# Two-layer retention and block-attention trunk: the weights' columns interleaved in memory by 16-byte lines, and read by TensorE in four strided passes

## The chip, the cores and the metric

The kernel runs as one program on one core of a Trainium2 chip. The metric is the device time of one execution in microseconds (us), and lower is better.

## What is computed

The reference is a decoder trunk of two layers over 256 tokens of width 1024, in float32. Cut to what matters here, it reads:

```python
for i in range(DEPTH):                                   # 2 layers
    h = rms_norm(x, norm_g[i])
    proj = h @ w_in[i]                                   # (256,1024) @ (1024,4096)
    rq, rk, rv, rz, mq, mk, mv, mz = jnp.split(proj, cuts, axis=-1)
    r_out = silu(rz) * retention(rotary(rq), rotary(rk), rv, ret_norm_g[i])
    m_out = silu(mz) * moba(rms_norm(mq, q_norm_g[i]), rms_norm(mk, k_norm_g[i]), mv, rel_bias)
    x = x + jnp.concatenate([r_out, m_out], -1) @ w_out[i]          # (1024,1024)
    gate = sigmoid(rms_norm(x) @ w_ple_gate[i])                     # (1024,1024)
    x = x + gate * rms_norm(p[i] @ w_ple[i], ple_norm_g[i])         # (256,1024)
```

With 256 tokens the block attention is plain causal attention inside one block, with a bias that depends on the distance of the two tokens. Nearly all arithmetic lies in the four weight products: `w_in`, `w_out`, `w_ple` and `w_ple_gate`.

## The kernel before

Tokens are handled in two row blocks of 128 (`m`), the width of 1024 in eight blocks of 128 (`k`), and output columns in groups of 512. To keep the precision of float32, each operand of a weight product is split into a high part (rounded to `fp32r`) and a low part (what is left), and three matmuls are added in PSUM: high by high, high by low, low by high. The function `mm3` (lines 364 to 372) issues these three. In each, the stationary operand is a 128x128 block of the activations (`a`), loaded into TensorE by an LDWEIGHTS that goes with each matmul, and the moving operand is 128 rows by 512 columns of the split weights (`wh` or `wl`), read in the order of its columns.

A weight travels in pieces of 512 KB (two `k` blocks of 512 columns). SyncE issues its load into one of eight staging buffers `wst` (line 320), ScalarE copies it to `wh` with rounding (line 330), VectorE subtracts to get `wl` (line 333), and TensorE then uses it for twelve matmuls. There are five `wh`/`wl` pairs; in some stretches buffers of the attention part (`T`, `V`, `G`, `PS`, `K2`) are lent to the weights as well, which is why the profile shows matmuls that read `T`, `G` or `K`. A last piece of the second layer is done with 256 columns at a time. The input projection of the first layer's first group starts from smaller loads (`in_early`), which `first_block`, `late_columns`, `key_block` and `first_rows` handle (lines 409 to 518): the first 128x512 block comes as two halves of 256 columns, its copy to `wh` is done in two casts (lines 427 and 444), and the first four real matmuls are 256 columns wide.

Between the weight products lie the attention and retention parts: small matmuls of 128 and 256 columns into `mix` (lines 894, 912, 922, 972), which read no weights. Activations are transposed by DMA on SyncE's queue (line 595).

The order of all instructions is set by a planner in the kernel itself, the class `Flow`, which keeps a clock for each engine. Each step of a chain says on which engine it runs, what it is assumed to cost, and what buffers it takes; the planner issues the steps in the order in which they would come ready. TensorE's clock moves by `ROW` for each matmul of 512 columns (`ROW = 0.227`, in us), by 0.53 of it at 256 columns in `mm3`, and by `TILE`, twelve rows, for the due time of a weight piece. The attention parts are put between the weight products by `tick()`, once their inputs have been ready, by the planner's clocks, for a margin. These costs decide the order of the instructions alone; on the chip semaphores hold each instruction until its inputs are there.

Of the kernel before, what the change touches and what calls it, by code (L numbers as in the profile page):

```python
# [52 lines left out]
PE, ACT, DVE, POOL, SP = range(5)  # L53
ROW = 0.227
TILE = 12 * ROW
# [182 lines left out]
def ask(eng, cost, take=(), after=(), mb=None):  # L238
    return eng, cost, take, after, mb
# [3 lines left out]
def tile_hybrid_trunk(ctx: ExitStack, tc: tile.TileContext, early, x, pT, ple_g, rel_bias,  # L243
# [106 lines left out]
    class Parts:  # L350
# [10 lines left out]
        def need(self, m, k):  # L361
            if (m, k) in self.made:
                flow.need(self.made.pop((m, k)))

    def mm3(ps, a, m, k, stage, kk, start, stop, cols=slice(0, GW)):
        a.need(m, k)
        wh, wl = stage.part(kk // 2)[kk % 2]
        ah, al = a.of(m, k)
        flow.row(3 * ROW * (1.0 if cols.stop - cols.start == GW else 0.53))
        nc.tensor.matmul(ps, ah, wh[:, cols], start=start, stop=False)  # L370
        nc.tensor.matmul(ps, ah, wl[:, cols], start=False, stop=False)  # L371
        nc.tensor.matmul(ps, al, wh[:, cols], start=False, stop=stop)  # L372

# [35 lines left out]
    def first_block(k, home, at):  # L409
        b = home[:, at:at + BLOCK]  # L410
        w = b[:, :GW] if k else home[:, at:at + 2 * FIRST].rearrange("p (t n) -> p t n", t=2)[:, :, :S]
        src = b[:, GW:] if k else home[:, at + S:at + 2 * S]
# [10 lines left out]
        if k:  # L423
            nc.scalar.copy(hi, w)
            firsts[k, "lo"] = flow.begin(first_low(k, w, hi, lo), k - 19.7, flow.end + HOP)
        else:
            nc.scalar.copy(hi[:, :S], w[:, 0])
            firsts["split"] = [v.rearrange("p (t n) -> p t n", t=2) for v in (hi, lo)]
        g = gains["g"][:, Q_NG + k:Q_NG + k + 1]
# [8 lines left out]
    def late_columns(home):  # L438
        w = home[:, :2 * FIRST].rearrange("p (t n) -> p t n", t=2)[:, :, :S]
        yield ask(SP, 0.43, mb=S / 2048)  # L440
        nc.sync.dma_start(w[:, 1], early_block("late"))
        yield ask(ACT, 0.36)
        hi, lo = firsts["split"]
        nc.scalar.copy(hi[:, 1], w[:, 1])
        firsts[0, "lo"] = flow.begin(first_low(0, w, hi, lo), -19.7, flow.end + HOP)
# [52 lines left out]
    def first_rows(k, ps, start, stop, key=()):  # L498
# [9 lines left out]
        for i, (which, w, c) in enumerate(order):  # L508
# [3 lines left out]
            for j, sl in enumerate([slice(0, S), slice(S, GW)] if halves else [slice(0, GW)]):  # L512
                if j:
                    flow.need(firsts["late"])
                for m in range(MT):
                    flow.row(0.12 if halves else ROW)
                    nc.tensor.matmul(ps[m][:, sl], (a0.lo if which[0] == "lo" else a0.hi)[:, k, m * P:(m + 1) * P],  # L517
                                     w[:, sl], start=start and i + j == 0, stop=stop and i == 2)

# [157 lines left out]
    def embed(l):  # L677
# [22 lines left out]
        for m in range(MT):  # L700
            ps = [bank(mix_p, "mix") for _ in range(2)]
            for n in range(2):
                for k, (wh, wl) in enumerate(w.part(n)):
                    ah, al = (v[:, k, m * P:(m + 1) * P] for v in (ph, pl))
                    flow.row(3 * ROW)
                    nc.tensor.matmul(ps[n], ah, wh, start=k == 0, stop=False)  # L706
                    nc.tensor.matmul(ps[n], ah, wl, start=False, stop=False)  # L707
                    nc.tensor.matmul(ps[n], al, wh, start=False, stop=k == 1)  # L708
                if m:
# [24 lines left out]
    def layer(l, aT):  # L734
        last = l == DEPTH - 1
        T, TC, V, G, VC, GC = {}, {}, {}, {}, {}, {}
        K2, Q2 = {}, {}

        def stats(m):
            return ST_X[l, m, "v"]  # L740
# [85 lines left out]
        def value(g, m, ps):  # L826
            yield ask(ACT, 0.585, take=() if m else ("V",), after=need_stats(m))
            if not m:
                V[g] = big.tile([P, MT, GW], F32, name="V", bufs=1)
            nc.scalar.activation(V[g][:, m], ps, AF.Copy, scale=stats(m)[0 if g == MV else 2])  # L830
            flow.free("acc")
# [432 lines left out]
```

## Time and profile before

| | |
|---|---|
| device time, median of 3 runs | 303.85 us (303.44 to 304.65) |
| the profiled execution: span from first to last instruction | 301.7 us |
| what lies around the span, against the median | 2.1 us (303.85 - 301.7) |
| granted TensorE clock over the span | 1.000 of full speed |
| TensorE matmuls, share of the span busy | 98% (1411 instructions) |
| VectorE, ScalarE, GpSimd busy | 84%, 72%, 11% |
| DMA, mean rate | 231 GB/s, 69.77 MB |

The profiled execution's own device time is not listed apart from the three runs, so its span is set beside their median, and the 2.1 us around it are taken as constant. In the rows of the profile, PE is TensorE's matmul, PEld its weight load (the stationary operand), DVE is VectorE, ACT ScalarE, POOL GpSimd, SP SyncE, and SPq the DMA issues on SyncE's queue. A matmul's time in a row runs from its start until its result is through; matmuls overlap, so what one costs in a row of them is the distance from one start to the next. A row such as `ACT wh L330 <- PE acc L372: 11.6, 13, 1.7` says that line 330 on ScalarE waited 11.6 us in all for line 372 on TensorE, 13 times, 1.7 us the longest.

### The profile page before, as it was taken

To read this page: it belongs to the slowest core of one execution; us is meant where nothing else is said; L and a number is where in the kernel's file an instruction comes from. 1 tells how busy PE (TensorE), PEld (TensorE's weight loads), DVE (VectorE), ACT (ScalarE), POOL (GpSimd) and SP (SyncE) were. 2 spreads that over 40 slices of the span, in tenths; PEclk is the share of its full clock that TensorE was granted. 3 is DMA by queue.
4 is the path that set the end of the run, shared out by engine and by line. 5 is a ranking of instruction groups with operands and counts; after the bars stand their busy time and mean duration, and the time that the engine had idled before them with its cause. 6 is when DMAs were issued, how large, how long until landed. Compare 5 with 4: busy or idle time off the path is not lost.

```text
span 301.7 us, 4301 instructions
## 1 busy us (share of the span) xinstructions
PE 296.9 (98%) x1411; PEld 248.5 (82%) x1411; DVE 253.6 (84%) x461; ACT 215.9 (72%) x376; POOL 32.5 (11%) x44
## 2 busy tenths in 40 slices
PE   8999999999999999999999999999999999999994
PEld 5888888888888888888888888888898888888884
DVE  4959799899899997899997489999978797969832
ACT  4789963889656985997793796699646869389211
POOL 6005200000001200031012220000000030002200
PEclk9999999999999999999999999999999999999999
DMA  7999989978769676896779769798997777833011
GB/s 236 366 405 411 276 241 379 303 243 184 237 205 297 266 194 228 179 295 245 250 198 293 243 187 227 258 218 175 281 323 184 252 223 185 276 73 70 1 72 70
DMA packets 61774, 69.77 MB, mean 231 GB/s; under 512 B 46260, under 2 KB 47160, under 8 KB 61624
## 3 DMA queue, kind: packets, MB, share of 16 engines
q1 hardware_dynamic: 61712, 69.50, 77.3%
q8 instruction: 11, 0.18, 0.2%
q14 instruction: 11, 0.09, 0.1%
q0 software_dynamic: 32, 0.01, 0.0%
q10 hardware_dynamic: 8, 0.00, 0.0%
HBM read 57.42 MB, written 1.05 MB: 194 GB/s over the span
## 4 chain that ended last, share of the span: by engine, by line
PE 98%; DVE 0%; ACT 0%; issue 0%
PE acc L371 26%; PE acc L372 26%; PE acc L370 26%; PE acc L517 5%; PE mix L922 4%; PE mix L894 2%; PE mix L278 1%; PE mix L708 1%; PE mix L707 1%; PE mix L371 1%; PE mix L370 1%; PE mix L372 1%; PE mix L706 1%; PE mix L972 1%; PE mix L912 1%; ACT tmp L1144 0%
## 5 line engine op out<-in xcount | busy, mean ns | idle before, releaser
L370 PE MATMUL acc<-wh,a 128*128 128x512 f32 (+1 forms) x286 | 110.4, 386 | 0.0
L371 PE MATMUL acc<-wl,a 128*128 128x512 f32 (+1 forms) x286 | 110.1, 385 | 0.0
L372 PE MATMUL acc<-wh,a 128*128 128x512 f32 (+1 forms) x286 | 110.0, 385 | 0.0
L333 DVE TENSOR_TENSOR wl<-wst,wh 128x1024 fp32r<-128x1024 f32 x76 | 91.8, 1217 | 10.4 <-ACT wh L330 10.3
L330 ACT CAST wh<-wst 128x1024 fp32r<-128x1024 f32 x76 | 79.5, 1057 | 21.3 <-PE acc L372 11.6
L372 PEld LDWEIGHTS acc<-wh,a 128*128 128x128 f32 x286 | 53.7, 188 | 10.6
L370 PEld LDWEIGHTS acc<-wh,a 128*128 128x128 f32 x286 | 53.8, 188 | 10.6
L371 PEld LDWEIGHTS acc<-wl,a 128*128 128x128 f32 x286 | 53.8, 188 | 10.5
L585 ACT COPY u<-tok 128x1024 uint16<-128x1024 uint16 x30 | 31.0, 1050 | 11.6 <-DVE tok L940 7.5
L637 POOL TENSOR_TENSOR ro<-rs_t,neghalf 128x4 f32<-128x4 f32 x4 | 5.8, 1459 | 132.2 <-DVE rs_t L635 132.2
L585 ACT COPY u<-x_t 128x1024 uint16<-128x1024 uint16 x12 | 12.5, 1041 | 8.2 <-DVE x_t L1100 6.3
L621 ACT CAST a<-tmp 128x512 fp32r<-128x512 f32 x20 | 12.4, 619 | 7.8 <-DVE tmp L618 5.8
L1144 ACT ACTIVATE tmp<-acc,hr 128x512 f32<-128x512 f32 (+1 forms) x9 | 5.8, 639 | 15.6 <-PE acc L372 15.6
L604 DVE COPY tmp<-w 128x512 uint16<-128x512 uint16 x40 | 16.1, 454 | 0.0
L604 DVE COPY T<-w 128x512 uint16<-128x512 uint16 x32 | 12.6, 455 | 2.2 <-DMA w<-u 2.2
L623 DVE TENSOR_TENSOR a<-tmp,a 128x512 fp32r<-128x512 f32 x20 | 13.7, 683 | 0.0
L1147 DVE SCALAR_TENSOR_TENSOR tmp<-tmp,E 128x512 f32<-128x512 f32 (+1 forms) x9 | 5.7, 629 | 8.5 <-ACT tmp L1144 8.5
L517 PE MATMUL acc<-wh,a 128*128 128x512 f32 (+1 forms) x42 | 11.7, 401 | 0.0
L922 PEld LDWEIGHTS mix<-V,PS 128*128 128x128 f32 x96 | 11.3, 192 | 0.3
L922 PE MATMUL mix<-V,PS 128*128 128x128 f32 x96 | 11.4, 275 | 0.0
L370 PE MATMUL acc<-T,a 128*128 128x512 f32 (+1 forms) x30 | 11.2, 375 | 0.0
L372 PE MATMUL acc<-T,a 128*128 128x512 f32 (+1 forms) x30 | 11.2, 375 | 0.0
(143 smaller groups left out, 462.3 us busy)
## 6 DMA issues: line engine op xcount, KB each, us to landing
wst<-in_w_in SPq DMA_DIRECT2D x59, 512.0 KB, 6.6
wst<-in_w_out SPq DMA_DIRECT2D x16, 512.0 KB, 7.4
wst<-in_w_gate SPq DMA_DIRECT2D x16, 512.0 KB, 4.3
wst<-in_w_ple SPq DMA_DIRECT2D x4, 512.0 KB, 7.6
wst<-in_early SPq DMA_DIRECT2D x4, 384.0 KB, 6.8
a<-in_early SPq DMA_DIRECT2D x3, 384.0 KB, 5.1
x_t<-in_x SPq DMA_DIRECT2D x1, 1024.0 KB, 11.7
gb<-in_ple_g SPq DMA_DIRECT2D x2, 512.0 KB, 7.2
```

The costliest lines, as they stand in the source:

```text
L330: nc.scalar.copy(hi, s)
L333: nc.vector.tensor_tensor(lo, s, hi.bitcast(F32), op=ALU.subtract)
L370: nc.tensor.matmul(ps, ah, wh[:, cols], start=start, stop=False)
L371: nc.tensor.matmul(ps, ah, wl[:, cols], start=False, stop=False)
L372: nc.tensor.matmul(ps, al, wh[:, cols], start=False, stop=stop)
L517: nc.tensor.matmul(ps[m][:, sl], (a0.lo if which[0] == "lo" else a0.hi)[:, k, m * P:(m + 1) * P], w[:, sl], start=start and i + j == 0, st ...
L585: nc.scalar.copy(u, src.bitcast(U16).rearrange("p (n t) -> p t n", t=2))
L604: nc.vector.tensor_copy(v, w[:, t].rearrange("p (h b) k -> p h (b k)", h=v.shape[1]))
L621: nc.scalar.copy(h, src)
L623: nc.vector.tensor_tensor(a.lo[:, k0:k0 + 4, m * P:(m + 1) * P], src, h.bitcast(F32), op=ALU.subtract)
L894: nc.tensor.matmul(ps, w[a], x[b], start=i == 0, stop=i == 2)
L922: nc.tensor.matmul(ps[:, h * DH:(h + 1) * DH], lhs(h, m, b), v[:, b, h * DH:(h + 1) * DH], start=b == 0, stop=b == m)
```

## The change

The weights hold the same numbers in another order. Before, the 512 columns of a piece lie one behind the other in each partition. Now the host cuts them into four column blocks of 128 (the lanes) and lays them by turns: four words (16 bytes) of the first block, four of the second, four of the third, four of the fourth, then the next four of the first, and so on. TensorE reads the moving operand in the old column order: the view `lanes` gives it an access pattern of three dimensions, block by block, and in a block line by line with a step of 64 bytes. A matmul of 512 columns thus reads its 2 KB in four passes, each over every fourth 16-byte line; one of 256 columns in two passes. The number, the width and the results of the matmuls stay, and so do the loads, casts and subtractions, but for the very first block: its two halves are now two lanes each, so that the two casts of 256 columns (lines 427 and 444 before) write, and the subtraction reads, runs of 8 words.

The planner's `ROW` goes from 0.227 to 0.22, and with it the planner's order. The step `value` gets a mark that keeps row block 1 from being planned ahead of row block 0, which allocates the tile; it is a rule of the planner and no instruction.

```diff
-ROW = 0.227
+ROW = 0.22
+LANES, LINE = 4, 4
...
+    def lanes(w):
+        return w.rearrange("p (l t n) -> p t l n", t=LANES, n=LINE)
+
+    def columns(w, sl):
+        return lanes(w)[:, sl.start // P:sl.stop // P]
+
     def mm3(ps, a, m, k, stage, kk, start, stop, cols=slice(0, GW)):
...
-        nc.tensor.matmul(ps, ah, wh[:, cols], start=start, stop=False)
-        nc.tensor.matmul(ps, ah, wl[:, cols], start=False, stop=False)
-        nc.tensor.matmul(ps, al, wh[:, cols], start=False, stop=stop)
+        wh, wl = columns(wh, cols), columns(wl, cols)
+        nc.tensor.matmul(ps, ah, wh, start=start, stop=False)
+        nc.tensor.matmul(ps, ah, wl, start=False, stop=False)
+        nc.tensor.matmul(ps, al, wh, start=False, stop=stop)
...
-            nc.scalar.copy(hi[:, :S], w[:, 0])
-            firsts["split"] = [v.rearrange("p (t n) -> p t n", t=2) for v in (hi, lo)]
+            firsts["split"] = [v.rearrange("p (l t n) -> p t l n", t=2, n=2 * LINE) for v in (hi, lo)]
+            nc.scalar.copy(firsts["split"][0][:, 0], w[:, 0])
...
-                                     w[:, sl], start=start and i + j == 0, stop=stop and i == 2)
+                                     columns(w, sl), start=start and i + j == 0, stop=stop and i == 2)
...
-                    nc.tensor.matmul(ps[n], ah, wh, start=k == 0, stop=False)
+                    nc.tensor.matmul(ps[n], ah, lanes(wh), start=k == 0, stop=False)
...
-            yield ask(ACT, 0.585, take=() if m else ("V",), after=need_stats(m))
+            yield ask(ACT, 0.585, take=() if m else ("V",), after=need_stats(m) + ((VA[g],) if m else ()))
...
+    def laned(w):
+
+        return w.reshape(*w.shape[:-1], -1, LANES, P // LINE, LINE).swapaxes(-3, -2).reshape(w.shape)
+
     def rows(w, n, half):
 
         L, K, N = w.shape
-        t = w.reshape(L, half, K // P // half, P, N // n, n)
+        t = laned(w).reshape(L, half, K // P // half, P, N // n, n)
```

The order of the instructions shifts at many places. Three of them follow; line numbers after 55 are higher in the changed kernel (370, 371, 372 become 378, 379, 380; 320 becomes 321; 595 becomes 604).

First, SyncE's queue in the first layer, where the first activations are transposed for the attention scores (`u` is the copy that is transposed into `w`; `tb` is the attention bias). Before:

```order
L320 DMA wst<-in_w_in 128x1024 x6
L572 DMA tb<-bd 128x4x256
L595 DMA_TRANSPOSE w_462<-u_417 128x8x128
L595 DMA_TRANSPOSE w_476<-u_439 128x8x128
L320 DMA wst<-in_w_in 128x1024 x2
L595 DMA_TRANSPOSE w_519<-u_493 128x8x128
L595 DMA_TRANSPOSE w_536<-u_513 128x8x128
L320 DMA wst<-in_w_in 128x1024 x11
```

and in the changed kernel:

```order
L321 DMA wst<-in_w_in 128x1024 x6
L604 DMA_TRANSPOSE w_429<-u_420 128x8x128
L581 DMA tb<-bd 128x4x256
L604 DMA_TRANSPOSE w_479<-u_443 128x8x128
L321 DMA wst<-in_w_in 128x1024
L604 DMA_TRANSPOSE w_514<-u_503 128x8x128
L321 DMA wst<-in_w_in 128x1024
L604 DMA_TRANSPOSE w_542<-u_512 128x8x128
L321 DMA wst<-in_w_in 128x1024 x12
```

The first transpose now stands ahead of the load of the bias, and one weight load stands between each two of the last three transposes.

Second, TensorE in the same stage: the attention scores of the first layer (into `mix`, from the heads' `T`, `K2` and `Q2`) between the projections. Before:

```order
L372 MATMUL acc<-wh,a 128x512
L912 MATMUL mix<-T 128x128 x4
L894 MATMUL mix<-K_579,Q_541 128x256 x12
L370 MATMUL acc<-wh,a 128x512
L371 MATMUL acc<-wl,a 128x512
```

and in the changed kernel:

```order
L380 MATMUL acc<-wh,a 128x512
L923 MATMUL mix<-T 128x128 x4
L905 MATMUL mix<-K_576,Q_547 128x256 x12
L378 MATMUL acc<-wh,a 128x512
L379 MATMUL acc<-wl,a 128x512
```

The neighbours read the same, but in TensorE's list the scores stand 12 rows further down: 12 matmuls of the projections that followed them now come ahead of them.

Third, SyncE's queue in the second layer, at transposes of the attention and retention part (`gb` is the gain of the embedding's norm). Before:

```order
L320 DMA wst<-in_w_in 128x1024 x6
L595 DMA_TRANSPOSE w_2146<-u_2128 128x8x128
L595 DMA_TRANSPOSE w_2167<-u_2141 128x8x128
L320 DMA wst<-in_w_in 128x1024 x2
L595 DMA_TRANSPOSE w_2224<-u_2175 128x8x128
L595 DMA_TRANSPOSE w_2241<-u_2214 128x8x128
L320 DMA wst<-in_w_in 128x1024
L595 DMA_TRANSPOSE w_2276<-u_2226 128x8x128
L595 DMA_TRANSPOSE w_2299<-u_2273 128x8x128
```

and in the changed kernel:

```order
L321 DMA wst<-in_w_in 128x1024 x6
L604 DMA_TRANSPOSE w_2150<-u_2135 128x8x128
L604 DMA_TRANSPOSE w_2176<-u_2164 128x8x128
L604 DMA_TRANSPOSE w_2198<-u_2186 128x8x128
L604 DMA_TRANSPOSE w_2224<-u_2208 128x8x128
L321 DMA wst<-in_w_in 128x1024
L604 DMA_TRANSPOSE w_2261<-u_2249 128x8x128
L321 DMA wst<-in_w_in 128x1024 x4
L297 DMA gb<-in_ple_g 128x1024
```

Four transposes now stand in a row where two weight loads parted them, and the weight loads come behind them.

More of the change, by code (lines that the diff above doesn't have):

```diff
@@ L410, in first_block @@
         b = home[:, at:at + BLOCK]
-        w = b[:, :GW] if k else home[:, at:at + 2 * FIRST].rearrange("p (t n) -> p t n", t=2)[:, :, :S]
+        w = b[:, :GW] if k else home[:, at:at + 2 * FIRST].rearrange("p (t n) -> p t n", t=2)[:, :, :S].rearrange("p t (l n) -> p t l n", n=2 * LINE)
         src = b[:, GW:] if k else home[:, at + S:at + 2 * S]
@@ L441, in late_columns @@
         nc.sync.dma_start(w[:, 1], early_block("late"))
+        w = w.rearrange("p t (l n) -> p t l n", n=2 * LINE)
         yield ask(ACT, 0.36)
@@ L705, in embed @@
                     flow.row(3 * ROW)
-                    nc.tensor.matmul(ps[n], ah, wh, start=k == 0, stop=False)
-                    nc.tensor.matmul(ps[n], ah, wl, start=False, stop=False)
-                    nc.tensor.matmul(ps[n], al, wh, start=False, stop=k == 1)
+                    nc.tensor.matmul(ps[n], ah, lanes(wh), start=k == 0, stop=False)
+                    nc.tensor.matmul(ps[n], ah, lanes(wl), start=False, stop=False)
+                    nc.tensor.matmul(ps[n], al, lanes(wh), start=False, stop=k == 1)
                 if m:
@@ L737, in layer @@
         K2, Q2 = {}, {}
+        VA = {g: Mark() for g in (MV, RV)}
         def stats(m):
@@ L826, in value @@
         def value(g, m, ps):
-            yield ask(ACT, 0.585, take=() if m else ("V",), after=need_stats(m))
+            yield ask(ACT, 0.585, take=() if m else ("V",), after=need_stats(m) + ((VA[g],) if m else ()))
             if not m:
                 V[g] = big.tile([P, MT, GW], F32, name="V", bufs=1)
+                flow.reach(VA[g])
             nc.scalar.activation(V[g][:, m], ps, AF.Copy, scale=stats(m)[0 if g == MV else 2])
@@ L1236 @@
     early = {k: blocks[k] for k in range(1, KT)}
-    early[0] = np.concatenate([blocks[0][:, :S], blocks[0][:, GW:], gains], 1)
-    early["late"] = blocks[0][:, S:GW]
+    sides = blocks[0][:, :GW].reshape(P, -1, 2, 2 * LINE).transpose(0, 2, 1, 3).reshape(P, 2, S)
+    early[0] = np.concatenate([sides[:, 0], blocks[0][:, GW:], gains], 1)
+    early["late"] = sides[:, 1]
     early |= {("K", k): w_in[0, MK, 0][:, k] for k in range(2)}
-    w_ple = a["w_ple"].reshape(DEPTH, 2, P, 2, GW).transpose(0, 2, 3, 1, 4).reshape(DEPTH, P, 4, GW)
+    w_ple = laned(a["w_ple"]).reshape(DEPTH, 2, P, 2, GW).transpose(0, 2, 3, 1, 4).reshape(DEPTH, P, 4, GW)
     arrays = {
```

## The prediction

> **What bounds the kernel now.** I read the page first, then the waits.
>
> ```profile
> span 301.7 us, 4301 instructions
> PE 296.9 (98%) x1411; PEld 248.5 (82%) x1411; DVE 253.6 (84%) x461; ACT 215.9 (72%) x376; POOL 32.5 (11%) x44
> PE 98%; DVE 0%; ACT 0%; issue 0%
> ```
>
> ```profile
> PE mix L278 <- PEq L1253: 0.8, 1, 0.8
> ACT wh L330 <- PE acc L372: 11.6, 13, 1.7
> SPq L320 <- DVE wl L333: 32.8, 21, 3.5
> ACT wh L330 <- DMA wst<-in_w_in: 3.7, 3, 1.9
> ```
>
> The chain that ended last lies on PE for 98% of the span. PE's only wait is 0.8 us at the start, and behind its last matmul there is only a short tail. The other three rows give the direction of pressure in the supply of weights: ACT's cast waits for PE to give a `wh` buffer back (11.6 us), the loads wait for DVE to empty a staging buffer (32.8 us), and only three times does a cast wait for a load (3.7 us). The weights stand ready and PE sets the pace; its time is the number of matmuls times the distance between their starts. So I read that distance off PE's order of time, at 512 columns (first and last of 132 matmuls in a row) and at 256 columns (first and last of 48).
>
> ```profile
> 18.64 0.39 PE L370 MATMUL acc<-wh,a 128*128 128x512 f32 x1
> ...
> 48.33 0.39 PE L372 MATMUL acc<-wh,a 128*128 128x512 f32 x1
> ...
> 291.78 0.28 PE L370 MATMUL acc<-wh,a 128*128 128x256 f32 x1
> ...
> 297.42 0.28 PE L372 MATMUL acc<-T,a 128*128 128x256 f32 x1
> ```
>
> At 512 columns it is (48.33 - 18.64) / 131 = 226.6 ns, at 256 columns (297.42 - 291.78) / 47 = 120.0 ns. The difference is 106.6 ns for 256 columns, 0.417 ns a column. 512 columns at that rate are 213.3 ns; 226.6 less that leaves **13.3 ns that each matmul pays whatever its width** (256 columns: 120.0 - 106.7, the same). This fixed part is the only thing that a different reading order could shorten, since the number of columns stays. Does another engine cause it?
>
> ```profile
> 200.00:210.00 10.00, 10.00 (x46) 8.29 (x45) 10.00 (x18) 10.00 (x15) 0.00 (x0) 1.00 0.85 181
> 280.00:290.00 10.00, 10.00 (x46) 8.29 (x45) 7.29 (x14) 1.79 (x3) 1.52 (x1) 1.00 0.04 15
> ```
>
> In these stretches of 10 us the columns are PE, PEld, DVE, ACT and POOL busy, the granted clock and the DMA share. With DVE and ACT busy throughout and DMA at 0.85, PE has 46 matmul records in the stretch; with ACT at 1.79 and DMA at 0.04 it has 46 too, at clock 1.00. So neither DVE, ACT nor DMA makes the fixed part. It lies inside TensorE: in its own two streams of reads, or in the switch from one matmul to the next.
>
> ```profile
> L370 PEld LDWEIGHTS acc<-wh,a 128*128 128x128 f32 x286 | 53.8, 188 | 10.6
> ```
>
> Each matmul has such a load of 128 words per partition beside it, which is 512 bytes, or 32 lines of 16 bytes. 13.3 ns are 13.3 / 0.417 = 32 columns' time. One column lost for each line that the weight load reads would be exactly that; it is a coincidence of numbers that suggests two read streams in each other's way, and no proof.
>
> **The change part by part.** The moving operand's order of addresses is the first and largest part. How many matmuls have it:
>
> ```profile
> wst<-in_w_in SPq DMA_DIRECT2D x59, 512.0 KB, 6.6
> wst<-in_w_out SPq DMA_DIRECT2D x16, 512.0 KB, 7.4
> wst<-in_w_gate SPq DMA_DIRECT2D x16, 512.0 KB, 4.3
> wst<-in_w_ple SPq DMA_DIRECT2D x4, 512.0 KB, 7.6
> ```
>
> ```profile
> 4.76 14.03 PE acc L517 x62
> ```
>
> The 59 + 16 + 16 + 4 = 95 pieces serve twelve matmuls each, 1140; the first blocks have 62; and 24 of the last products are cut in two, which adds 24: 1226 in all. Of these 48 + 4 = 52 have 256 columns (line 517 starts with four such), 1174 have 512. All lie on the path that sets the end.
>
> What one gains has no row, since no matmul of before reads in strides. Its best end is the whole fixed part, 13.3 ns: 1226 x 13.3 = 16.3 us. Its end at nothing is a fixed part that is the switch between matmuls. Beyond nothing there is a loss: 512 columns now come in four passes with three seams (256 columns: one), and a seam could cost as much as a matmul's own fixed part: (1174 x 3 + 52) x 13.3 = 47.5 us. I take half of the fixed part, 6.7 ns, the middle between the gains' ends: if the two streams meet in the memory, a stream that stays on every fourth line should leave the other free part of the time, and nothing in the rows says how large a part. The planner's new order is laid for the same distance (220 ns for 226.6), so at that value nothing needs to be reordered; this is no evidence that it comes. The sum: 1226 x 6.7 = **8.2 us less**.
>
> [...]
>
> The first block's casts and its subtraction now handle runs of 8 words.
>
> ```profile
> 3.58 0.41 ACT L427 CAST wh<-a 128x256 fp32r<-128x256 f32 x1 [1.36 <-DMA a<-in_early]
> 3.93 0.41 ACT L444 CAST wh<-a 128x256 fp32r<-128x256 f32 x1
> ...
> 4.13 1.50 PEld L517 LDWEIGHTS acc<-wh,a 128*128 128x128 f32 x6 [0.28 <-ACT wh L427]
> ```
>
> PE's first weight load waits for the first cast, so its length is on the path. If runs of 8 words were half as fast it would cost 0.4 us; I take 0.1, as the words within a run are consecutive. The subtraction has no row of such a pattern either; PE needs it only after four more matmuls. The mark in `value` costs nothing, being no instruction.
>
> The planner's order moves. A faster PE asks for each weight piece earlier, by 6.7 / 226.6 = 3% of the time since the start. The tightest piece is the first that lines 330 and 333 make:
>
> ```profile
> 16.40 1.23 DVE L333 TENSOR_TENSOR wl<-wst,wh 128x1024 fp32r<-128x1024 f32 x1 [1.30 <-ACT wh L330]
> 18.86 0.39 PE L371 MATMUL acc<-wl,a 128*128 128x512 f32 x1
> ```
>
> It is done at 17.63 and used at 18.86, 1.2 us later; by then PE gains 62 x 6.7 ns = 0.4 us, so it holds. The scores of the first layer stand 12 matmuls later in PE's list, 12 x 0.22 = 2.6 us of other work, which covers the transposes that also moved on SP's queue (one now ahead of the bias load; weight loads put between three others). In the second layer four transposes stand in a row, and two weight loads of 512 KB come behind them; if a transpose there waits for its copy on ACT, those loads wait too, and behind them DVE and PE. The eight staging buffers lie in between. I price all such new waits on PE at 0.3 us, after the one wait for another engine that a weight load shows (0.28); the bounds are 0 and the 2.9 us worked out under the second rival. The tail behind the last matmul stays.
>
> Sum against the profiled execution: 301.7 - 8.2 + 0.1 + 0.3 = 293.9 us of span; with the 2.1 us around it 296.0, which is 303.85 - 7.8.
>
> **The rivals.** *The fixed part is the switch between matmuls.* Then the order of addresses is all the same to it, and the change does not do what it could be for. For: 13.3 ns appear at 512 and at 256 columns alike, as a switch would. Against: no row excludes the two streams, and 32 columns for 32 lines fit them. Time: 303.85 + 0.1 = 304.0. [...]
>
> *VectorE becomes the bound.* PE gets its 6.7 ns, but where DVE is full it cannot go faster.
>
> ```profile
> 40.00:50.00 10.00, 10.00 (x52) 8.52 (x51) 10.00 (x17) 5.29 (x6) 0.00 (x0) 1.00 0.95 314
> 60.00:70.00 10.00, 10.00 (x46) 8.28 (x45) 9.59 (x14) 9.09 (x17) 0.00 (x0) 1.00 0.81 226
> 90.00:100.00 10.00, 10.00 (x58) 8.74 (x57) 9.89 (x29) 7.38 (x11) 1.41 (x2) 1.00 1.01 314
> 130.00:140.00 10.00, 10.00 (x45) 8.27 (x45) 9.54 (x20) 8.40 (x13) 3.65 (x3) 1.00 0.99 330
> 140.00:150.00 10.00, 10.00 (x46) 8.26 (x45) 9.90 (x15) 7.33 (x10) 0.00 (x0) 1.00 0.67 194
> 150.00:160.00 10.00, 10.00 (x46) 8.29 (x45) 9.83 (x22) 8.31 (x16) 2.11 (x2) 1.00 0.76 205
> 190.00:200.00 10.00, 10.00 (x56) 8.65 (x55) 9.90 (x15) 7.99 (x21) 0.00 (x0) 1.00 0.80 236
> 210.00:220.00 10.00, 10.00 (x46) 8.29 (x45) 10.00 (x17) 6.76 (x9) 0.00 (x0) 1.00 0.99 282
> 270.00:280.00 10.00, 10.00 (x46) 8.26 (x45) 9.62 (x21) 10.00 (x21) 2.08 (x2) 1.00 0.28 53
> ```
>
> With 200 to 210 these are ten stretches in which DVE (fourth number after the stretch's name, after PE and PEld) is at 95% or more, 100 us; 3% of them is 2.9 us that would be lost of the 8.2. Against: between them DVE falls to 73% (280 to 290), and the waits above say that the weights run ahead. Time: 296.0 + 2.9 - 0.3 = 298.6. It is faster than now all the same, and inside the forecast's own range.
>
> *The seams cost.* [...] If a seam costs one line, four columns or 1.7 ns, and nothing is gained, it is (1174 x 3 + 52) x 1.7 = 6.1 us more: 303.85 + 6.1 + 0.1 = 310.0; at 13.3 ns it would be 351. The forecast's gain is eaten up from 8.2 us / 3574 = 2.3 ns a seam. For: a jump of address in the midst of a matmul occurs nowhere in before. Against: inside a pass the step is as regular as before, and the seam is known beforehand from the pattern.
>
> **How the numbers follow.** A measurement of this kernel can tell about 0.5%, 1.5 us, from no change (the three runs lie 1.2 us apart); that is 1.5 us / 1226 = 1.2 ns a matmul net. The forecast, that a part of the fixed 13.3 ns goes, has 0.68, and with VectorE as the bound 0.08 more; both are faster, 0.76. That the fixed part is the switch has 0.12; that the seams cost has 0.12. The forecast's own range is a loss of 4 to 11 ns a matmul: 303.85 - 4.9 + 0.4 = 299.4 down to 303.85 - 13.5 + 0.1 = 290.4. To hold 8 in 10, the range must reach to the switch's 304.0 and its 0.5 us of new waits at most, and at the low end to 290. It leaves out the seams and a fixed part that goes nearly whole (287.5 to 290): 290.0 to 304.5 us, forecast 296.0.
>
> **What would show it.** In PE's order of time the distance of two starts of 512 columns should be 220 ns where it was 226.6, and at 256 columns 113 where it was 120; the sum of the span follows from that. If the distance shortens and the span doesn't, the waits of PE must show lines 333 or 330, and the second rival holds. If the distance stays at 226.6, the fixed part is the switch; if at 512 columns it lengthens by three times what it does at 256, the seams cost. A weight load (PEld) shorter or longer than 188 ns would show that the two streams do meet. The forecast is wrong if the distance is over 225.4 ns or under 213.

## The result and the profile after

The changed kernel takes 305.66 us (median of 5 runs, 305.48 to 307.07) against 303.85 before: a ratio of 1.0068, 95% interval 1.0045 to 1.0090. It is slower by 1.8 us, where 7.8 us less were forecast. The profiled execution took 305.6 us, with a span of 303.7. One execution of `before_shifted` below took 376.61 us at a granted clock of 0.756 and is not counted in its time.

The page of the changed kernel, its span, its engines and the engines of the chain that ended last:

```profile
span 303.7 us, 4292 instructions
PE 296.6 (98%) x1411; PEld 247.3 (81%) x1411; DVE 255.9 (84%) x461; ACT 215.7 (71%) x376; POOL 32.3 (11%) x44
PE 92%; DVE 3%; DMA 2%; ACT 1%; issue 1%; SPq 0%; DVEq 0%
```

The totals hardly differ. What differs is the chain: PE carried 98% of it and now carries 92%. PE's waits in the changed kernel name who took the place:

```profile
PE acc L378 <- DVE tok L1049: 1.3, 1, 1.3
PE mix L279 <- PEq L1269: 0.8, 1, 0.8
PE acc L380 <- DVE a L632: 0.4, 1, 0.4
PE acc L378 <- ACT a L630: 0.2, 1, 0.2
```

Three of PE's four waits are new (the 0.8 us at the start stood there before). And from the waits of ScalarE:

```profile
ACT wh L331 <- PE acc L380: 21.3, 22, 1.9
```

The casts of the weights wait longer for PE than before (21.3 us for 11.6), so the weights' supply isn't what is late.

First the distances. PE's order of time in the changed kernel, the first and last start of three rows of matmuls (144 at 512 columns, 345 at 512, 48 at 256):

```profile
18.70 0.39 PE L378 MATMUL acc<-wh,a 128*128 128x512 f32 x1
...
50.64 0.38 PE L380 MATMUL acc<-wh,a 128*128 128x512 f32 x1
...
115.75 0.38 PE L378 MATMUL acc<-V,a 128*128 128x512 f32 x1
...
193.71 0.39 PE L380 MATMUL acc<-wh,a 128*128 128x512 f32 x1
...
293.63 0.28 PE L378 MATMUL acc<-wh,a 128*128 128x256 f32 x1
...
299.12 0.27 PE L380 MATMUL acc<-wh,a 128*128 128x256 f32 x1
```

These are (50.64 - 18.70) / 143 = 223.4 ns, (193.71 - 115.75) / 344 = 226.6 ns and (299.12 - 293.63) / 47 = 116.8 ns, where before had 226.6 and 120.0. The same instructions with the same shapes thus run at two distances in one kernel. Row by row they don't scatter but repeat: 230, 224, 221, 218 ns in the first stretch, and 220, 222, 221, 234, 239, 225, 226 in the second. Over all rows of 512 columns the mean is 226.0 ns (1151 distances; before 226.9).

Then the holes. The two places in PE's order where it stood still:

```profile
107.52 0.39 PE L380 MATMUL acc<-wh,a 128*128 128x512 f32 x1
109.22 0.49 PE L378 MATMUL acc<-wh,a 128*128 128x512 f32 x1 [1.32 <-DVE tok L1049]
109.56 0.39 PE L379 MATMUL acc<-wl,a 128*128 128x512 f32 x1
...
113.80 0.38 PE L380 MATMUL acc<-T,a 128*128 128x512 f32 x1
114.33 0.49 PE L378 MATMUL acc<-V,a 128*128 128x512 f32 x1 [0.16 <-ACT a L630]
114.67 0.38 PE L379 MATMUL acc<-PS,a 128*128 128x512 f32 x1
115.42 0.49 PE L380 MATMUL acc<-V,a 128*128 128x512 f32 x1 [0.37 <-DVE a L632]
115.75 0.38 PE L378 MATMUL acc<-V,a 128*128 128x512 f32 x1
```

From 107.52 to 109.56 two distances take 2.04 us in place of 0.45, and from 113.80 to 115.75 four take 1.95 in place of 0.91: 1.6 + 1.0 = 2.6 us of holes. Set against 1151 x 0.87 ns = 1.0 us and 0.15 us at 256 columns that the distances save, this gives +1.5 of the +2.0 us of span. About 0.3 more lie in the first 19 us: line 378 begins at 18.70 (before 18.64), although the matmuls ahead of it had run at 223.4 ns too. There a weight load waited for a cast of the early weights, and that cast for its own load from memory:

```profile
PEld acc L526 <- ACT wh L432: 0.6, 1, 0.6
```

```profile
6.88 0.62 ACT L432 CAST wh<-a 128x512 fp32r<-128x512 f32 x1 [1.36 <-DMA a<-in_early]
```

That wait of the cast is 0.59 us in before, and 0.60 and 0.89 us in two kernels that follow (`layout_alone`, `order_alone`). The last 0.2 us lie behind the last matmul: from its end to the end of the span it is 4.29 us, and 4.05 in before.

Why was line 1049 late? It is the gate of the retention's output, reads the PSUM bank that line 378 is to fill, and needs the tile `T` that line 1021 on ScalarE writes. ScalarE (ACT), VectorE and TensorE in the changed kernel; line 933 is the retention's own product (the first row of its 24 matmuls):

```profile
93.52 0.49 PE L933 MATMUL mix<-V,PS 128*128 128x128 f32 x3
```

```profile
104.72 1.07 ACT L331 CAST wh<-wst 128x1024 fp32r<-128x1024 f32 x1
105.66 0.84 ACT L1021 ACTIVATE T<-mix,mr,ro 128x128 f32<-128x128 f32 x2
106.36 1.08 ACT L594 COPY u<-tok 128x1024 uint16<-128x1024 uint16 x1
107.29 0.85 ACT L1021 ACTIVATE T<-mix,mr,ro 128x128 f32<-128x128 f32 x2
```

```profile
106.22 2.36 DVE L334 TENSOR_TENSOR wl<-wst,wh 128x1024 fp32r<-128x1024 f32 x2
108.49 0.68 DVE L1049 TENSOR_TENSOR tok<-T,acc 128x512 f32<-128x512 f32 x1
```

The same three steps in before:

```profile
91.32 0.38 PE L922 MATMUL mix<-V,PS 128*128 128x128 f32 x2
```

```profile
104.86 1.49 ACT L1010 ACTIVATE T<-mix,mr,ro 128x128 f32<-128x128 f32 x4
```

```profile
106.38 0.69 DVE L1038 TENSOR_TENSOR tok<-T,acc 128x512 f32<-128x512 f32 x1 [0.65 <-ACT T L1010]
```

Before, the four heads of row block 1 were normalised in one go from 104.86, and the gate ran at 106.38. Now the product starts 2.2 us later, the heads are done in two pairs with a copy between them and a cast ahead, and behind them VectorE has two weight subtractions (2.36 us) ahead of the gate, which runs at 108.49, 2.1 us later. PE's list reached the matmul that needs the bank without such a delay. The second hole waits for the high and low parts of activations (lines 630 and 632), which are made from the gate's output `tok` after its transpose.

### The profile page after: what moved, and what is told of

Same layout as the page of the kernel before. It is cut to its first block, busy times and chain, and to the rows that moved or that the text cites. A ratio compares the mean times of both kernels' runs of the same rounds, so it can differ in the third digit from the quotient of the medians.

```text
span 303.7 us, 4292 instructions
## 1 busy us (share of the span) xinstructions
PE 296.6 (98%) x1411; PEld 247.3 (81%) x1411; DVE 255.9 (84%) x461; ACT 215.7 (71%) x376; POOL 32.3 (11%) x44
## 4 chain that ended last, share of the span: by engine, by line
PE 92%; DVE 3%; DMA 2%; ACT 1%; issue 1%; SPq 0%; DVEq 0%
PE acc L380 25%; PE acc L378 25%; PE acc L379 25%; PE acc L526 4%; PE mix L933 4%; PE mix L905 2%; DMA a<-in_early 2%; DVE wl L334 2%; PE mix L716 1%; PE mix L715 1%; PE mix L717 1%; PE mix L378 1%; PE mix L380 1%; PE mix L379 1%; PE mix L983 1%
## 5 line engine op out<-in xcount | busy, mean ns | idle before, releaser
L331 ACT CAST wh<-wst 128x1024 fp32r<-128x1024 f32 x78 | 81.2, 1057 | 30.7 <-PE acc L380 21.3
L334 DVE TENSOR_TENSOR wl<-wst,wh 128x1024 fp32r<-128x1024 f32 x78 | 94.0, 1220 | 9.9 <-ACT wh L331 9.7
L378 PEld LDWEIGHTS acc<-wh,a 128*128 128x128 f32 x292 | 54.8, 188 | 12.1 <-DVE tok L1049 1.7
L380 PEld LDWEIGHTS acc<-wh,a 128*128 128x128 f32 x292 | 54.8, 188 | 10.7
L379 PEld LDWEIGHTS acc<-wl,a 128*128 128x128 f32 x292 | 54.8, 188 | 10.3
L594 ACT COPY u<-tok 128x1024 uint16<-128x1024 uint16 x30 | 30.9, 1049 | 8.8 <-DVE tok L831 4.4
L646 POOL TENSOR_TENSOR ro<-rs_t,neghalf 128x4 f32<-128x4 f32 x4 | 6.9, 1734 | 133.7 <-DVE rs_t L644 133.7
L380 PE MATMUL acc<-T,a 128*128 128x512 f32 x28 | 10.8, 387 | 0.0
L378 PE MATMUL acc<-T,a 128*128 128x512 f32 x28 | 10.8, 386 | 0.0
```

What stands on the lines that cost most here:

```text
L331: nc.scalar.copy(hi, s)
L334: nc.vector.tensor_tensor(lo, s, hi.bitcast(F32), op=ALU.subtract)
L378: nc.tensor.matmul(ps, ah, wh, start=start, stop=False)
L379: nc.tensor.matmul(ps, ah, wl, start=False, stop=False)
L380: nc.tensor.matmul(ps, al, wh, start=False, stop=stop)
L594: nc.scalar.copy(u, src.bitcast(U16).rearrange("p (n t) -> p t n", t=2))
```

## The experiments

Two theories were open. By the first, the layout gains and the planner's new order loses more; by the second, the layout itself loses. And for the distance: does it come from the two operands' addresses, or from the switch between matmuls?

### The layout without the order, and the order without the layout

```diff
 layout_alone: the changed kernel
-ROW = 0.22
+ROW = 0.227
```

> The changed layout with ROW back at 0.227, so that the instructions stand in the order of before. Theory (the lost time is the order's: waits on TensorE between 107 and 116 us and at the start): no waits of TensorE beyond those of before; 512-column matmuls at 223.4 ns up to the first attention scores and 226.6 behind them, so about 0.5 to 1 us less than before, ratio 0.997 to 0.999. Rival (the layout itself brings the waits, by casts or reads that are slower): waits of 2 us or more on TensorE here too, ratio 1.005 or more.

It took 301.67 us, ratio 0.9932 (0.9917 to 0.9948); PE has none of the new waits. PE's order of time in this kernel, the ends of two stretches (431 and 227 matmuls of 512 columns):

```profile
93.78 0.39 PE L379 MATMUL acc<-wl,a 128*128 128x512 f32 x1
...
189.83 0.38 PE L380 MATMUL acc<-wh,a 128*128 128x512 f32 x1
...
238.33 0.38 PE L379 MATMUL acc<-wl,a 128*128 128x512 f32 x1
...
289.54 0.40 PE L380 MATMUL acc<-T,a 128*128 128x512 f32 x1
```

That is 96.05 / 430 = 223.4 ns and 51.21 / 226 = 226.6 ns: the same two distances, but at other places than expected, and over a longer stretch. The layout alone gains 2.0 us, where 0.5 to 1 us were expected.

```diff
 order_alone: the kernel before
-ROW = 0.227
+ROW = 0.22
 and the mark in value (VA), as in the change
```

> The layout and the contiguous reads of before, with ROW 0.22 and the mark in the value step, so that the instructions stand in the order of the changed kernel. Theory (the order costs): 226.7 ns throughout and the waits of the changed kernel at 107 to 116 us, some 2 to 3 us more than before, ratio 1.007 to 1.012. Rival (the layout costs): no new waits, ratio 1.000 within 0.002.

It took 306.55 us, ratio 1.0089 (1.0074 to 1.0103), with the weights laid out and read as before. Its waits on PE:

```profile
PE acc L370 <- DVE tok L1040: 1.3, 1, 1.3
PE mix L278 <- PEq L1255: 0.8, 1, 0.8
PE acc L372 <- DVE a L623: 0.4, 1, 0.4
```

These are the waits of the changed kernel but for its smallest, under the line numbers of before. So the order costs 2.8 us by itself, and the first theory holds. The parts sum to -2.0 + 2.8 = +0.8 us, and the change measures +1.8. Part of the rest shows in the distances: their mean is 225.4 ns in layout_alone and 226.0 in the changed kernel, which over 1151 is 0.7 us. The last 0.3 us are within the uncertainty of the three measurements, and the start and the tail of the span differ by as much (0.3 and 0.2 us above).

### What the distance depends on

Three kernels hold no trunk: rows of matmuls on one pair of fp32r operands, and a pause between the rows.

```diff
 micro_reads: 42 matmuls a row
+ps[:, :n] += stationary.T @ moving     # 128 x 128 by 128 x n
 moving:     contiguous; l4, l2, l8, l16 (by turns of 4, 2, 8, 16 blocks); 256, 384 columns; bf16
 stationary: one or two lines of 16 bytes further on; every second or fourth word; 64 columns
```

> No trunk at all: rows of 42 matmuls each on one stationary and one moving tile, in 19 forms, a pause ahead of each row; the output is one PSUM bank and zeros. Theory (the fixed part of 13.3 ns is the weight load's reads meeting the moving reads, one column's time for each 16-byte line that the load reads): contiguous 226.7 ns; stationary with step 2 (64 lines) 240, step 4 (128 lines) more still; 64 stationary columns (16 lines) 220; bf16 (16 lines) 220; 384 and 256 columns 173 and 120. Strided moving operand after a pause 223.4 in a cycle of four, after narrow matmuls 226.7 in a cycle of seven. Rival (the fixed part is the switch between matmuls): 226.7 at all 512-column forms with contiguous moving operand, whatever the stationary operand's step, width or type.

Mean distance over the second half of each row, in ns:

```
contiguous 512 / 384 / 256 columns            226.7 / 173.4 / 120.0
strided l4, 512 / 256 columns                 227.0 / 115.3
strided l2 / l8 / l16                         233.4 / 246.7 / 278.1
l4, passes read from the last to the first    223.4
l4, stationary one / two lines on             230.0 / 226.8
contiguous, moving operand one line on        231.7
contiguous, stationary every 2nd / 4th word   233.4 / 235.0
contiguous, stationary of 64 columns          229.6
contiguous, bf16                              215.8
```

The weight loads in the profile of this kernel, grouped by line (stationary of every fourth word, contiguous, and of 64 columns):

```profile
L109 PEld LDWEIGHTS pb<-mv,st 128*128 128x128 f32 x42 | 9.9, 310 | 0.8 <-ACT st L52 0.8
...
L68 PEld LDWEIGHTS pa<-mv,st 128*128 128x128 f32 x42 | 7.8, 188 | 2.3 <-ACT st L52 0.8
...
L112 PEld LDWEIGHTS pa<-mv,st 128*64 128x64 f32 x42 | 5.6, 134 | 4.5 <-ACT st L52 0.7
```

A load of half the columns takes 134 ns in place of 188, and the matmuls don't come closer (229.6 for 226.7); where it takes 310 ns they stand only 8 ns further apart. The expected 223.4 ns behind a pause did not come either: the strided row ran in the sequence of seven (227.0). So "one column lost for each line that the weight load reads" falls. But the distance changes when only an operand's address changes (231.7 ns for 226.7 with the moving operand one line on), which speaks against a mere switch between matmuls.

```diff
 micro_entry: 32 matmuls a row
+k matmuls of 128 columns just ahead of a row (k = 1, 2, 3, 5, 8)
 further lines of offset, reversed lines, other block sizes
```

> No trunk: rows of 32 matmuls in further forms, the output is one PSUM bank and zeros. Strided rows in the old and in reversed pass order, entered after 1, 2, 3, 5 or 8 matmuls of 128 columns without a pause; then other orders of lines and other offsets between the two operands. Theory (two read streams whose meeting depends on the phase at which a row is entered): the forward order settles at 223.4 or at 226.7 depending on what stood ahead of the row, each within 0.3 ns; the reversed order at 223.4 always; an offset of one line costs 3 to 5 ns in either, an offset of four lines nothing. Rival (the cycle belongs to the form, not to the phase): one value for each form whatever stands ahead of it.

The strided row runs at 223.3 ns behind one or two narrow matmuls, at 226.6 behind three or eight, at 227.2 behind five (the same sequence of seven, cut at another place). Read from the last pass to the first it runs at 222.2 in all of these but behind two narrow ones (226.8). PE's order of time, the row behind one narrow matmul and that behind three, from the fifth matmul on (28 matmuls each; the second number is the time from the first's start to the last's end):

```profile
23.43 6.43 PE L79 MATMUL pb<-mv,st 128*128 128x512 f32 x28
...
55.42 6.51 PE L95 MATMUL pb<-mv,st 128*128 128x512 f32 x28
```

Less one matmul of 0.38 us, these are 6.05 / 27 = 224 and 6.13 / 27 = 227 ns. How these rows were entered decided which of the two repeating sequences they fell into, and they stayed in it. That would explain two distances in one kernel, and that a new order brings others. One row had a steady 220.0 ns: l4 with the stationary operand three lines further on. The expectation that an offset of four lines costs nothing failed: contiguous reads with the moving operand two, three and four lines on take 233.3, 233.3 and 228.9 ns. Reversed passes with the stationary operand one, two and three lines on take 221.7, 226.7 and 220.2. The contiguous lines read backwards, without any offset, take 233.3.

```diff
 reversed_passes: the changed kernel with ROW = 0.227
-w.rearrange("p (l t n) -> p t l n", t=LANES, n=LINE)
+w.rearrange("p (l t n) -> p t l n", t=LANES, n=LINE)[:, ::-1]
 and the host lays the four blocks in the opposite order
```

> The changed layout with the four passes read last to first (the host lays the blocks so that the result is the same), ROW 0.227, so the order of before. Theory (the reversed order has the short cycle alone): 223.4 ns in all stretches, 1226 x 3.3 = 4.0 us less than before, ratio 0.987, and 2 us less than the layout alone. Rival (entry decides here too): stretches of 226.7 remain and the ratio is that of the layout alone, 0.993.

It took 300.86 us (299.54 to 301.65), ratio 0.9902 (0.9882 to 0.9923). In the profiled execution the mean distance is 226.8 ns up to 80 us and 222.3 from 94 us on (781 distances), 223.6 over all, against layout_alone's 225.4. That execution is the fastest of the six (299.54), 1.3 us below their median, so its mean is not that of the median, and the ratio is only 0.003 below layout_alone's. It is again a matter of entry.

### Is it ROW?

```diff
 row_0_2255, row_0_2235: the changed kernel
-ROW = 0.22
+ROW = 0.2255   /   0.2235
```

> The changed kernel with ROW 0.2255, near the distance that was measured over its span (226.0). Theory (the loss is the planner's wrong row): the waits of TensorE at 107 to 116 us are gone or under 0.5 us, ratio 0.992 to 0.995. Rival (any new order costs, being another draw): waits of 1 us or more, ratio over 1.000.

302.65 us (301.50 to 303.84), ratio 0.9958 (0.9942 to 0.9975). In the profiled execution three holes remain, of 505, 741 and 561 ns from start to start, at 112.9, 113.7 and 138.6 us: 1.1 us more than three plain distances. It is the slowest of the seven (303.84); whether the faster ones have these holes, no trace shows.

> The changed kernel with ROW 0.2235, the shorter of the two measured cycles. Theory (the loss grows with the distance of ROW from the measured 226): some of the waits, 0.5 to 1.5 us, ratio 0.995 to 1.001. Rival (any order other than that of 0.22 is as good): no waits, ratio 0.993.

303.75 us (302.83 to 304.43), ratio 0.9993 (0.9981 to 1.0005). In the profiled execution PE waits nowhere but at the start, and the long stretch from 92 to 192 us runs at 226.6 ns. The ratio is the one that the theory gave, but the waits behind it, 0.5 to 1.5 us, are not in this trace, which shows longer distances in their place. The execution is one of the fastest of the twelve (302.87). With one trace from the slow end and one from the fast end, the two runs don't settle whether the holes grow with ROW's distance from the measured one. What they show is that each value of ROW gives another order, with its own entries.

### The operands' addresses

```diff
 micro_offsets: 28 matmuls a row
+stationary = st[:, 4 * j:4 * j + 128]      # j lines of 16 bytes on, j = 0 to 31
```

> No trunk: rows of 28 matmuls, each row with the stationary tile's start moved by some 16-byte lines (0 to 31) against the moving tile's, with strided and with contiguous moving reads; the output is one PSUM bank and zeros. Theory (what the distance costs is where the two read streams meet): with strided reads the distance repeats every four lines of offset, 220.0 at +3, +7, +11 and so on, 230 at +1, 227 at +2; with contiguous reads another row of values, 226.7 at 0. Rival (the 220.0 at +3 was a matter of entry): no period, values scattered between 220 and 235.

PE's order of time for four of its rows: strided with offset 0 and 3, contiguous with offset 0 and 4 (26, 25, 25 and 26 matmuls):

```profile
14.99 6.04 PE L68 MATMUL pa<-mv,st 128*128 128x512 f32 x26
...
36.68 5.67 PE L77 MATMUL pb<-mv,st 128*128 128x512 f32 x25
...
185.43 5.83 PE L140 MATMUL pa<-mv,st 128*128 128x512 f32 x25
...
214.33 6.23 PE L152 MATMUL pa<-mv,st 128*128 128x512 f32 x26
```

Less one matmul of 0.38 to 0.40 us: 5.65 / 25 = 226, 5.29 / 24 = 220, 5.44 / 24 = 227 and 5.83 / 25 = 233 ns. All rows, over their second half:

```
strided, offset in lines   0     1     2     3     4     5     6     7
                         227.2 229.1 226.9 220.0 227.0 224.8 226.5 225.4
                           8     9    10    11    12    13    14    15
                         225.2 226.7 220.0 223.2 220.0 223.1 225.1 224.1
                          16    19    20    23    24    27    28    31
                         225.7 220.0 226.9 226.1 224.5 223.3 220.0 225.6
contiguous                 0     1     2     3     4     5     6     7
                         226.6 233.4 233.5 233.3 233.5 231.8 234.2 233.3
                           8     9    10    11
                         233.7 233.2 233.2 230.5
```

The pattern repeats after 16 lines, not after four: 3 and 19, 12 and 28, 11 and 27 agree, and at 0 and 16, 4 and 20, 7 and 23, 8 and 24, 15 and 31 the distances run through the same sequence, number by number (their means differ by up to 1.5 ns where the half row cuts a sequence). The offset was moved by the stationary operand alone; no run moves both operands together, so it isn't shown that only the difference of the two addresses counts. Strided rows reach a steady 220.0 at offsets 3, 10 and 12; contiguous ones have their best at offset 0, which is where the kernel before has its operands. The change took the strided reads at the same offset 0, where they run at 223.4 or 226.6 by their entry.

```diff
 shifted_old_order: the changed kernel with ROW = 0.227 (order of before)
 shifted_new_order: the changed kernel with ROW = 0.22 (its own order)
 before_shifted:    the kernel before, its weights contiguous
+gap(48) ahead of the activations' buffers, gap(16) behind   # words per partition; 192 and 64 bytes, 12 lines
 before_shifted: gap(16) ahead, gap(48) behind               # 4 lines
```

> The changed layout, ROW 0.227 (the order of before), and 192 unused bytes ahead of the activation tiles and 64 behind them, so that the stationary operand starts 12 lines of 16 bytes on against the weights; the 48 embedding matmuls keep their old offset. Theory (the distance is set by the offset modulo 16 lines, 220.0 at +12): 220.0 ns in all stretches, 1178 x 6.7 = 7.9 us less than before, ratio 0.974, and no new waits, since the weights run 1.2 us or more ahead. Rival (in the trunk other engines' accesses or the entry undo it): distances of 223 to 227, ratio 0.985 to 0.993.

299.04 us, ratio 0.9830 (0.9817 to 0.9842). PE's order of time in it, the ends of two stretches (132 and 126 matmuls):

```profile
18.49 0.39 PE L387 MATMUL acc<-wh,a 128*128 128x512 f32 x1
...
48.41 0.38 PE L389 MATMUL acc<-wh,a 128*128 128x512 f32 x1
...
191.71 0.39 PE L387 MATMUL acc<-wh,a 128*128 128x512 f32 x1
...
219.22 0.39 PE L389 MATMUL acc<-wh,a 128*128 128x512 f32 x1
```

29.92 / 131 = 228.4 and 27.51 / 125 = 220.1 ns; a third kind of stretch runs at 223.3, and the mean over all is 222.6. So the expected 220.0 everywhere did not come: with these operands, too, the distance falls into one of several sequences, and in the first stretch into a slower one than in before. One new hole of 0.5 us stands at the gate (line 1058). This version beats both kernels all the same: before took 304.24 us beside it, 5.2 us more.

> The changed kernel with the same shift, ROW 0.22, its own order. Theory (that order was laid for 220 ns; where the chip runs at 220 it has no waits to speak of): ratio 0.970 to 0.976, as with the old order. Rival (the order itself is a bad draw): the waits at 107 to 116 us remain, 2 to 3 us, ratio 0.981 to 0.984.

301.16 us, ratio 0.9902 (0.9889 to 0.9914). The mean distance is the same 222.6 ns, so what parts it from the run above, 2.1 us, is the order's. Its longest wait on PE:

```profile
PE acc L387 <- DVE tok L1058: 1.4, 1, 1.4
```

> The kernel before, contiguous reads, with 64 unused bytes ahead of the activation tiles and 192 behind them, so that the stationary operand starts 4 lines on; nothing else is changed. Theory (two read streams in each other's way): 233.5 ns for 226.7, 1178 x 6.8 = 8.0 us more, ratio 1.026. Rival (the fixed part is the switch between matmuls): ratio 1.000.

311.30 us, ratio 1.0228 (1.0215 to 1.0241). Nothing was changed but the addresses (two small memsets fill the gaps). PE's order of time, the ends of a stretch of 431 matmuls:

```profile
97.41 0.39 PE L380 MATMUL acc<-wl,a 128*128 128x512 f32 x1
...
197.62 0.39 PE L381 MATMUL acc<-wh,a 128*128 128x512 f32 x1
```

100.21 / 430 = 233.0 ns, as the small kernel had it at offset 4. The fixed part of a matmul follows the addresses in the trunk too; the rival "it is the switch" is out.

### What in the order costs the 2.6 us

In TensorE's list of the first layer the four attention groups begin at rows 173, 307, 315 and 334 before, and at 185, 331, 339 and 346 in the change (counted in matmuls ahead of them: 203, 355, 393 and 423, and 215, 379, 417 and 435). Two margins put them back, with ROW at 0.22:

```diff
 groups_back: the changed kernel
-groups.append(([both(TC, MQ, MK), lambda: [L_B]], moba_scores, 3, 2.9))
+groups.append(([both(TC, MQ, MK), lambda: [L_B]], moba_scores, 3, 0.3))
-               moba_out, 3, 2.0))
+               moba_out, 3, 0.3))
 groups_back_shifted: the same with the gaps of shifted_new_order
```

> The changed kernel with ROW at 0.22, and the margins of two attention groups, moba_scores and moba_out, at 0.3 (2.9 and 2.0 in the change). In the first layer the four attention groups then stand in TensorE's list where they stand before the change (rows 173, 307, 315, 334; in the change 185, 331, 339, 346), and ScalarE's list around the retention's normalisation reads as before the change. Theory 1: the wait of 1.3 us of line 378 on line 1049 comes from the groups' place. It and the holes beside it (2.7 us in all at 107 to 116 us) shrink to under 1 us, and the ratio to before is 0.991 to 0.999. Theory 2: the loss comes from the rest of the new order (casts, copies and transposes that also moved). Then line 378 still waits over 1 us for line 1049, and the ratio is 1.004 or more. The distances of the starts are not foreseen, since each order enters its rows in another way; they are read from the trace and taken apart from the waits.

302.52 us, ratio 0.9957 (0.9943 to 0.9971). All that is left on PE is the wait at the start, and ScalarE normalises row block 1 in one go again (the waits of this kernel, and its ScalarE and VectorE in order of time):

```profile
PE mix L279 <- PEq L1269: 0.8, 1, 0.8
```

```profile
105.08 1.50 ACT L1021 ACTIVATE T<-mix,mr,ro 128x128 f32<-128x128 f32 x4
```

```profile
106.61 0.69 DVE L1049 TENSOR_TENSOR tok<-T,acc 128x512 f32<-128x512 f32 x1 [0.54 <-ACT T L1021]
```

> As groups_back, with the activations moved by twelve lines of 16 bytes (as in shifted_new_order, which took 0.990 of before, and shifted_old_order, 0.983). Theory 1, the groups' place: the wait of 1.4 us for line 1058 goes, and the ratio is 0.983 to 0.986, that of the old order. Theory 2, the rest of the new order: the wait stays and the ratio is 0.989 or more. A ratio between would say that the place makes a part of it.

299.08 us, ratio 0.9844 (0.9829 to 0.9859), mean distance 222.5 ns, no new wait on PE: the shifted old order's time again (0.9830), within the intervals. The groups' place makes the holes, with what the planner moves along with it: the margins are the only edit, but ScalarE's and VectorE's orders follow. It isn't the only thing that can: at ROW 0.2255 the last three of the four groups stand where they stood before (the first six matmuls later), and its trace has 1.1 us of smaller holes; at 0.2235 the last group stands six matmuls earlier than before, and its trace has none.

## Why the prediction was wrong, point by point

**What bounds the kernel.** Right: PE sets the pace, its time is the number of matmuls times their distance, and no other engine makes the fixed part of 13.3 ns: in the two shifted trunks the distance changes with an address alone (233.0 ns in a long stretch of `before_shifted` for 226.6 in before; a mean of 222.6 in `shifted_old_order` for 225.4 in `layout_alone`). In the profiled executions without holes the span closely followed the distance (301.7, 299.6 and 297.1 us at means of 226.9, 225.4 and 222.5 ns in before, `layout_alone` and `groups_back_shifted`).

**"1226 x 6.7 = 8.2 us less".** The idea was right in kind and the term mis-sized. The fixed part does depend on where the operands lie: moving the activations by four lines, with nothing else changed, costs 6 ns a matmul (233.0 for 226.6 in `before_shifted`). But the value taken, half of 13.3 ns, was the middle between ends and rested on no row. Measured are 0.9 ns at 512 columns and 3.2 ns at 256 in the changed kernel: 1.0 + 0.15 us, and 2.0 us for the layout alone. The step that failed is "a stream that stays on every fourth line should leave the other free part of the time". That was my estimate of a cause, and no run shows it; the runs show distances alone, a steady 220.0 ns at 3, 10 and 12 lines in the small kernel, and 223.4 or 226.6 at offset 0, where the change keeps the operands. That 220.0 is the forecast's own value is chance. The number 32 for 32 columns and 32 lines was a coincidence, as the prediction said it might be: with half the columns to load the distance was 229.6 ns, not less than 226.7.

**"A loss of 4 to 11 ns a matmul."** No run shows the 11 of the range's low end: no fp32r row of 512 columns came below 220.0 ns, 6.7 under the contiguous 226.7, and bf16, which the weight products don't use, ran at 215.8. Nor did either order have one distance of its own: contiguous reads run at 226.6 at offset 0 and at 233.5 at 4, strided ones at 223.3 to 227.2 at offset 0 and at 220.0 at 3, and the contiguous lines read backwards at 233.3. The stationary operand's address alone moves the distance by 9 ns (220.0 to 229.1 strided).

**"The scores of the first layer stand 12 matmuls later ... which covers the transposes."** This step failed for what follows the scores. I looked at what the groups wait for and not at who waits for them. Not the scores alone had moved, but the whole row of groups, the two in the middle by 24 rows and the last by 12 (334 to 346), and at its end stand the normalisation, the gate, and the PSUM bank that the next weight product needs. The new waits, priced at 0.3 us "after the one wait for another engine that a weight load shows", are 2.6 us. That this is near the upper bound of 2.9 is chance: the bound was a price of VectorE's full stretches. Putting the groups back takes them away.

**"At that value nothing needs to be reordered."** Wrong: the order was laid for 220 ns, the matmuls ran at 226, and the order lost 2.8 us on matmuls of before and 2.1 us on those that ran at 222.6. The mismatch of ROW and distance is not needed for this loss: at 222.6 ns it was nearly as large, and with the groups put back it went at the same ROW.

**The first casts and the tightest piece.** No row of waits of lines 330 or 333 (now 331, 334) on PE's side appeared, and the tightest piece holds. The casts that write runs of 8 words cost nothing: they take 0.41 us each as before and start at 3.59 and 3.93 us (before 3.58 and 3.93). The 0.3 us of the start come from a later load.

**"What would show it."** By its own sign (over 225.4 ns) the forecast is wrong at 226.0. Two other signs would have misled: a distance that stays near 226.6 was to mean the switch, which `before_shifted` rules out (233.0), and a weight load other than 188 ns was to show that the two streams meet, but in `micro_reads` it takes 188 and 187 ns with the stationary operand one and two lines on (lines 97 and 100), while the matmuls stand 230.0 and 226.8 apart.

**The rivals.** "The switch" gave 304.0 us, the nearest time, but by a cause that before_shifted rules out. "VectorE becomes the bound" didn't occur: in `groups_back_shifted`, at 222.5 ns, PE waits for nothing but its start. "The seams cost" isn't needed, and no run shows its 1.7 ns a seam: four passes at the right offset run at 220.0, 6.7 ns under one pass. More blocks do cost (278 ns at sixteen), and so do two (233), which no count of seams orders.

**The sum as measured.** The layout -2.0 us, the order +2.8, together +0.8; the other entries of the new order into its rows +0.7; and 0.3 that no run separates: +1.8. The span of the profiled execution, 2.0 us longer, is made up of 2.6 of holes, 0.3 at the start and 0.2 in the tail, less 1.15 that the distances save.

Open is why the distances repeat in sequences of four or seven, and why 16 lines are the period; no run separates the difference of the two addresses from each address by itself. Which entry leads into which sequence was seen, not predicted. The best offset for the reversed passes was not tried in the trunk.

## What to carry to other kernels

When PE is the bound, measure the distance of matmul starts for the pair of operands as they lie in memory: moving one of them by a few 16-byte lines was worth more here than the new layout (3 us more and 7 us lost, for 2 us by the layout). Judge a planner's reordering apart from the change that came with it, by running the old order with the new code and the new order with the old code; a group that moves later in the bound engine's list is to be followed to whoever waits for its result and its buffers. A value between two far bounds with no row near it is no forecast; a small kernel with one row of the new access would have given it.

## What the runs showed of the hardware that was not expected

- An fp32r matmul of 128x128 by 512 columns in a row takes 220.0 to 278.1 ns from start to start with the same arithmetic, by the addresses and strides of its two operands (`micro_offsets`, `micro_reads`); bf16 takes 215.8.
- The stationary operand's start against the moving one's counts, with strided reads with a period of 16 lines (256 bytes): 220.0 ns at 3, 10 and 12 lines in the small kernel; in the trunk 12 lines gave 220.1, 223.3 or 228.4. Contiguous reads take 226.6 at 0 and 230.5 to 234.2 at 1 to 11 lines; no run goes further.
- Rows of equal strided matmuls fall into repeating sequences of distances (four: mean 223.4; seven: mean 226.6), and in `layout_alone` the mean of the first held over 431 matmuls; in `micro_entry` what ran just ahead decided which (223.3 behind one narrow matmul, 226.6 behind three). Contiguous rows ran at 226.7 behind a pause and behind narrow matmuls alike.
- A weight load of every fourth word takes 310 ns in place of 188, and the matmuls beside it stand 8 ns further apart.
